# x read in two layouts, and the first pair's projection three token tiles ahead of its attention

## The chip, the cores and the metric

The kernel runs on one core of a Trainium2 chip. The metric is the device time of one execution in microseconds (us); the time before is the median of three runs.

## What is computed

A decoder trunk of two residual layers on x of 1024 tokens by 1024 features, all in float32. Layer 0 mixes tokens with gMLP (A) and with a mixture of dilated sliding-window attentions (B); layer 1 with gated linear attention; each layer ends in a gated MLP with a causal convolution. The change touches the beginning of layer 0. Cut to that, the reference is:

```python
h = rms_norm(x, norm_mix_g[layer]).astype(x.dtype)        # x * rsqrt(mean(x*x) + EPS) * g
z = h @ w_in                                              # columns u, v, q, k, vb
a_out = chunked_gmlp(gelu(u), gelu(v), a_ln_g, a_ln_b, a_ws, a_bs)
qh = rms_norm(heads(q), q_g)                              # 8 heads of 64
kh = rms_norm(heads(k), k_g)
vh = heads(vb).astype(jnp.float32)
for window, dilation in B_BRANCHES:                       # ((128, 1), (512, 4), (2048, 16))
    o_r, l_r = dilated_branch(qh, kh, vh, window, dilation)
...
x = x + concat([a_out, b_out]) @ w_out
x = x + conv_ffn(rms_norm(x, norm_ffn_g[layer]), ...)
```

## The kernel before, in words

Tokens are handled in NT = 8 tiles of P = 128. Every large product is done in three passes over operands that are split into a high and a low part (`split`, L98 to L101: ScalarE writes the high part as float32r, VectorE the rest; `scaled`, L103, does the same for weights and multiplies by a gain). The `hq` tiles hold the split, feature-major x of all tokens: `hq[g][n // 4]` has the four feature blocks of parity g for four token tiles.

**Stage 1, `even` (L509).** For each token tile n, x is loaded token-major (L523), its eight 128x128 blocks are transposed on TensorE into PSUM tiles `pt` (L530), and `split` puts them into `hq` (L531). ScalarE squares the same tile with a running sum (L536), and GpSimd makes of it the reciprocal root mean square `r0[:, n]` (`inv_rms`, L137). r0 isn't applied to `hq`, but to the projections' results.

**Stage 2, `attention` (L643).** The eight heads are four pairs. `project(p)` (L696) has, per token tile, one projection `pj` of 24 matmuls (8 feature blocks in 3 passes, 384 columns: q, k, v of a pair), the QK-norm of its result (L712 to L718: ScalarE, VectorE, GpSimd), the values `vN` (L720, also stored to DRAM, L721), the split of q and k, their transposes `tq` and `tk` (L730, L738), and one attention `unit` of the undilated branch (L670): scores `sc`, exponential on ScalarE (L667), transposes `pP` (L681), and products with the values `po` (L689). `dilated(p)` (L757) is eight more units, `combine` weighs the two. `project(p + 1)` is written behind `dilated(p)`. PSUM's eight banks are: `pt` 2, `sc` 2, `pj` 2, `po` 1, `tq` 1 (L512); `pt` serves x's transposes and `pP`. `qn` has 2 buffers, `vN` 3.

**Stage 3.** `gmlp` (projections `pv`) and `u_proj` (`pu`), 8 tiles of 24 matmuls with 512 columns each, then the output projection and the rest of the trunk.

The program is built with a scheduler that fixes the order of the instructions on each engine; loops are where it starts from, not what stands in the queue at the end. All loads and stores go out from SyncE's queue (SP), in order.

## Time and profile before

| | us |
|---|---|
| median of 3 runs (2170.96 to 2174.12) | 2171.78 |
| the profiled execution | 2173.38 |
| its span, from the first to the last instruction | 2171.7 |
| TensorE (PE) busy | 2138.3 |
| VectorE (DVE) busy | 1533.7 |
| ScalarE (ACT) busy | 1033.9 |
| GpSimd (POOL) busy | 488.9 |

The profile is of one execution. PE's weight loads are shown apart (PEld). An idle time carries the engine that ended it. A timeline merges like instructions: start, length, engine, line, name and count; where the length of a merged row reaches over the start of the next, that is the latency of its last instruction. In a row of a window, `(x66)` counts instructions, and PEclk is the granted TensorE clock as a share.

### The profile page before, as it was taken

How to read it: one execution, taken by the hardware profiler on the slowest of the kernel's cores; microseconds unless marked ns; L12 is line 12 of the kernel's file. 1: busy time of each engine (PE TensorE's matmuls, PEld its weight loads, DVE VectorE, ACT ScalarE, POOL GpSimd, SP SyncE). 2: the span in 40 equal slices, each digit the busy share in tenths (PEclk: the TensorE clock that was granted, in tenths of full speed). 3: DMA queues.
4: the chain of work that ended last, by engine and by line, in shares of the span. 5: the costliest groups of instructions: out<-in, count | busy, mean ns of one | idle time of the engine just before them, and what ended most of it. 6: DMA issues, size and time to landing. Idle time of an engine off the chain costs nothing.

```text
span 2171.7 us, 29864 instructions
## 1 busy us (share of the span) xinstructions
PE 2138.3 (98%) x10508; PEld 1811.4 (83%) x10508; DVE 1533.7 (71%) x2451; ACT 1033.9 (48%) x1998; POOL 488.9 (23%) x519
## 2 busy tenths in 40 slices
PE   8999999999999999999999999999999999999999
PEld 7999988887888888878889888888788888888887
DVE  6566655577887888755577776667788878885554
ACT  6555545355444444444454455534544444444443
POOL 4444411012342434100020011110233424220000
PEclk9999999999999999999999999999999999999999
DMA  4122312655444444675563233386554444457555
GB/s 163 43 83 62 82 51 84 217 207 193 159 151 160 160 165 160 199 266 195 193 215 127 73 98 97 107 295 232 197 165 160 151 152 157 165 181 276 199 196 202
DMA packets 157254, 349.59 MB, mean 161 GB/s; under 512 B 17408, under 2 KB 54272, under 8 KB 156720
## 3 DMA queue, kind: packets, MB, share of 16 engines
q1 hardware_dynamic: 157104, 347.68, 47.6%
q8 instruction: 83, 1.36, 0.3%
q14 instruction: 67, 0.55, 0.1%
HBM read 239.02 MB, written 108.59 MB: 160 GB/s over the span
## 4 chain that ended last, share of the span: by engine, by line
PE 87%; DVE 4%; DMA 4%; ACT 3%; issue 1%; POOL 0%; SPq 0%; ACTq 0%; DVEq 0%; POOLq 0%
PE puB L290 11%; PE pgB L290 11%; PE pv L190 6%; PE pgC L290 6%; PE puC L290 6%; PE pj L190 5%; PE pdB L397 5%; PE pdC L397 5%; PE po L190 4%; PE pdO L397 4%; PE puA L290 3%; PE pgA L290 3%; PE pdP L397 2%; PE pdQ L397 2%; PE pu L190 2%; PE pBq L992 2%
## 5 line engine op out<-in xcount | busy, mean ns | idle before, releaser
L101 DVE TENSOR_TENSOR da<-ar,da 128x512 fp32r<-128x512 f32 x154 | 106.2, 690 | 160.2 <-ACT da L100 160.1
L100 ACT CAST da<-ar 128x512 fp32r<-128x512 f32 x154 | 95.9, 623 | 215.0 <-PE pdQ L397 91.8
L190 PE MATMUL po<-wo,hq 128*128 128x512 f32 x768 | 184.3, 395 | 1.2 <-ACT hq L100 1.2
L190 PEld LDWEIGHTS po<-wo,hq 128*128 128x128 f32 x768 | 141.6, 188 | 30.9 <-ACT hq L100 1.6
L190 PE MATMUL pv<-wv,hq 128*128 128x512 f32 (+2 forms) x768 | 139.8, 339 | 2.0 <-DVE b L1024 1.6
L397 PE MATMUL pdB<-dw,da 128*128 128x512 f32 x528 | 136.3, 391 | 2.4 <-ACT dw L100 1.7
L397 PE MATMUL pdC<-dw,da 128*128 128x512 f32 x528 | 135.8, 390 | 0.0
L190 PEld LDWEIGHTS pv<-wv,hq 128*128 128x128 f32 x768 | 118.9, 189 | 17.4 <-DVE b L1024 2.1
L397 PEld LDWEIGHTS pdB<-dw,da 128*128 128x128 f32 x528 | 98.6, 188 | 24.0 <-ACT dw L100 2.1
L190 PE MATMUL pj<-wq,hq 128*128 128x384 f32 x576 | 117.3, 346 | 0.2 <-ACT vN L720 0.2
L256 POOL TENSOR_TENSOR S1g<-rg 128x512 f32<-128x512 f32 x20 | 30.0, 1498 | 382.9 <-DMA wsd<-D 249.7
L397 PEld LDWEIGHTS pdC<-dw,da 128*128 128x128 f32 x528 | 99.1, 188 | 20.5
L101 DVE TENSOR_TENSOR dw<-wr,dw 128x512 fp32r<-128x512 f32 x154 | 105.6, 686 | 8.2 <-ACT dw L100 7.7
L140 POOL TENSOR_SCALAR rn<-ssq 128x1 f32<-128x1 f32 x24 | 9.6, 399 | 452.2 <-ACT h L148 246.0
L397 PE MATMUL pdO<-dw,da 128*128 128x512 f32 x396 | 102.3, 389 | 0.2 <-DVE dw L101 0.2
L190 PEld LDWEIGHTS pj<-wq,hq 128*128 128x128 f32 x576 | 100.3, 191 | 0.5 <-ACT vN L720 0.4
L100 ACT CAST dw<-wr 128x512 fp32r<-128x512 f32 x154 | 95.0, 617 | 11.9 <-DMA wr<-in_w_dn 5.0
L397 PEld LDWEIGHTS pdO<-dw,da 128*128 128x128 f32 x396 | 74.3, 188 | 15.9 <-DVE dw L101 0.6
L319 DVE SCALAR_TENSOR_TENSOR t<-g,cw,t 128x1022 f32<-128x1022 f32 x44 | 76.6, 1742 | 0.1
L318 DVE SCALAR_TENSOR_TENSOR t<-g,cw,t 128x1023 f32<-128x1023 f32 x44 | 60.2, 1368 | 16.3 <-ACT t L317 16.3
L303 DVE TENSOR_TENSOR g<-g,s1g 128x512 f32<-128x512 f32 x22 | 16.2, 737 | 76.7 <-ACT s1g L302 76.7
L320 ACT ACTIVATE t<-t 128x1024 f32<-128x1024 f32 x44 | 46.7, 1061 | 32.5 <-DVE t L319 32.5
(1073 smaller groups left out, 5458.7 us busy)
## 6 DMA issues: line engine op xcount, KB each, us to landing
ar<-actd SPq DMA_DIRECT2D x70, 512.0 KB, 3.6
rd<-in_w_down SPq DMA_DIRECT2D x44, 512.0 KB, 3.7
wsd<-D SPq DMA_DIRECT2D x88, 256.0 KB, 2.5
rg<-in_w_gate SPq DMA_DIRECT2D x42, 512.0 KB, 3.6
ru<-in_w_up SPq DMA_DIRECT2D x42, 512.0 KB, 4.7
wr<-wsd SPq DMA_DIRECT2D x40, 512.0 KB, 4.3
actd<-t SPq DMA_DIRECT2D x66, 256.0 KB, 2.2
wr<-in_w_dn SPq DMA_DIRECT2D x30, 512.0 KB, 4.6
```

Of the source, the lines that this page charges most:

```text
L100: (hi or A.copy)(dst[0], src)
L101: (lo or V.tensor_sub)(dst[1], src, f32(dst[0]))
L140: G.tensor_scalar(r, ssq, 1.0 / n, EPS, op0=ALU.mult, op1=ALU.add)
L190: T.matmul(o, L[i], R[jj][:, sl], start=(k == 0 and (ii, jj) == PASSES[0]), stop=(k == nk - 1 and (ii, jj) == PASSES[-1]))
L256: G.tensor_tensor(sums[name], x, y, op=op)
L290: T.matmul(o, L[ii][:, j * P : j * P + P], right[p][:, jj, j, :], skip_group_check=more, start=(not more and j == 0 and (ii, jj) == PASSES ...
L303: V.tensor_add(C22, C22, s1)
L318: V.scalar_tensor_tensor(t[:, 1:], g[:, : S - 1], w(1), t[:, 1:], op0=ALU.mult, op1=ALU.add)
L319: V.scalar_tensor_tensor(t[:, 2:], g[:, : S - 2], w(0), t[:, 2:], op0=ALU.mult, op1=ALU.add)
L320: A.activation(t, t, AF.Silu)
L397: T.matmul(o, L[ii][:, t * P : t * P + P], R[jj], skip_group_check=more, start=start and not more and (ii, jj) == PASSES[0], stop=stop and ...
L992: T.matmul(o, L[ii][:, j * P : j * P + P], right[p][:, jj, j, :], skip_group_check=more, start=(not more and j == 0 and (ii, jj) == PASSES ...
```

## The change

The host hands x over a second time, as `x_T`: for each token tile the eight blocks already feature-major, in the order that `hq` wants. Stage 1 loads a tile of `x_T` and splits it straight from SBUF; the 64 transposes of x and their PSUM tiles are gone. For tiles 0 and 1, GpSimd writes the high part of the second half. The token-major x is loaded as well, for the row statistics alone, which are taken in place: of tiles 0 to 2 in stage 1, of tile n + 3 behind the values of projection n.

`project` is split: `projected(n)` has the projection, the QK-norm and the values, and for pair 0 it is called three tiles ahead of the units (`lead = 3`); tiles 1 and 3 of pair 0 use `pt` banks, so that four projections can be under way. For all pairs `qn` now has 5 buffers and `vN` 6, the values are taken before the norm, and the gains `gqk` are kept once and broadcast over the two heads instead of being loaded twice.

```diff
@@ -518,26 +518,57 @@
             wx = par0.enter_context(tc.tile_pool(name="wx", bufs=4, side="right", reuse_waits="tile"))
             pq0 = par0.enter_context(tc.tile_pool(name="pq0", bufs=1, side="right", reuse_waits="tile"))
             with tc.tile_pool(name="nrm", bufs=1, reuse_waits="tile") as pool:
+                Q.dma_start(g0, a["norm_mix_gT"])
+                xk = pq.tile([P, 4, S], F32, tag="kT", bufs=1, name="xk")
+                xq = pq.tile([P, 2, S], F32, tag="qR", bufs=1, name="xq")
+
+                def home(name, tag, bufs):
+                    return pool.tile([P, D], F32, tag=tag, bufs=bufs, name=name)
+
+                def statistics(n, xt):
+                    ssq = small.tile([P, 1], F32, tag="ssq", name=f"ssq{n}")
+                    A.activation(xt, xt, AF.Square, accum_out=ssq)
+                    inv_rms(ssq, 1, D, f"rn{n}", r0[:, n : n + 1])
+
+                def token_rows(n):
+                    xt = home(f"x0{n}", "a", 5) if n < 2 else xk[:, n - 2] if n < 6 else xq[:, n - 6]
+                    Q.dma_start(xt, rows(a["x"], n))
+                    later.append(xt)
+                    if n < 3:
+                        statistics(n, xt)
+
+                later = []
                 for n in range(NT):
-                    xt = pool.tile([P, D], F32, tag="x", bufs=3, name=f"x0{n}")
-                    Q.dma_start(xt, rows(a["x"], n))
+                    xt = home(f"xf{n}", "a", 5) if n < 4 else home(f"xf{n}", "b", 2) if n < 6 else xq[:, n - 6]
+                    xf = xt.rearrange("p (g j t) -> p g j t", g=2, j=4)
+                    Q.dma_start(xf, a["x_T"][n])
+                    for g in range(2):
+                        split(place(hq[g][n // 4], n), xf[:, g], hi=G.tensor_copy if g and n < 2 else None)
                     if n == 0:
-                        Q.dma_start(g0, a["norm_mix_gT"])
-                    for g in range(2):
-                        pt = ps.tile([P, 4, P], F32, tag="pt", name=f"pt{n}{g}")
-                        for j in range(4):
-                            k = 2 * j + g
-                            T.transpose(pt[:, j, :], xt[:, k * P : (k + 1) * P], ident)
-                        split(place(hq[g][n // 4], n), pt)
-                    if n == 1:
                         wq0 = load_qkv(0, wx)
-                    h = pool.tile([P, D], F32, tag="h", bufs=2, name=f"h{n}")
-                    ssq = small.tile([P, 1], F32, tag="ssq", name=f"ssq{n}")
-                    A.activation(h, xt, AF.Square, accum_out=ssq)
-                    inv_rms(ssq, 1, D, f"rn{n}", r0[:, n : n + 1])
+                        token_rows(0)
+                    elif n > 1:
+                        if n == 2:
+                            gqk = gains(pq)
+                        token_rows(n - 1)
+                token_rows(NT - 1)
+
+            def rest(n, ins):
+                if n < 5:
+                    with tc.issue_after(ins.ins):
+                        statistics(n + 3, later[n + 3])
+
             with tc.tile_pool(name="at", bufs=2, reuse_waits="tile") as at, \
                     tc.tile_pool(name="av", bufs=1, reuse_waits="tile") as av:
-                return attention(ps, at, av, pq, pq0, par0, wx, wq0, masks, gm_open)
+                return attention(ps, at, av, pq, pq0, par0, wx, wq0, gqk, masks, rest, gm_open)
+
+    def gains(pq):
+
+        gqk = pq.tile([P, 2, 64], F32, name="gqk", bufs=1)
+        Q.dma_start(gqk[:, 0], a["q_g"].partition_broadcast(P))
+        Q.dma_start(gqk[:, 1], a["k_g"].partition_broadcast(P))
+        V.tensor_scalar(gqk[:, 0], gqk[:, 0], -0.125, None, op0=ALU.mult)
+        return gqk
 
     def band_masks(pool):
 
@@ -640,14 +671,8 @@
 
         proj512(ps, load_half(a["w_vu"][1], "wu", g0), "pu", consume)
 
-    def attention(ps, at, av, pq, pq0, par0, wx, wq0, masks, gm_open):
-
-        gqk = pq.tile([P, 2, 2, 64], F32, name="gqk", bufs=1)
-        for s in range(2):
-            Q.dma_start(gqk[:, 0, s, :], a["q_g"].partition_broadcast(P))
-            Q.dma_start(gqk[:, 1, s, :], a["k_g"].partition_broadcast(P))
-        V.tensor_scalar(gqk[:, 0], gqk[:, 0], -0.125, None, op0=ALU.mult)
-        gqk = gqk.rearrange("p a s c -> p (a s c)")
+    def attention(ps, at, av, pq, pq0, par0, wx, wq0, gqk, masks, rest, gm_open):
+
         mband, mboth = masks
 
         def by4(t):
@@ -693,7 +718,7 @@
             return (at.tile([P, 4, 132], F32, tag="ot", name="ot" + name, bufs=5),
                     ps.tile([P, 4, P], F32, tag="po", name="po" + name))
 
-        def project(p, ws=None, then=None):
+        def project(p, ws=None, then=None, early=None):
 
 
             ws = ws or load_qkv(p, wx)
@@ -701,24 +726,38 @@
             qR = pool.tile([P, 2, S], F32R, tag="qR", bufs=1, name=f"qR{p}")
             kT = pool.tile([P, 4, S], F32R, tag="kT", bufs=1, name=f"kT{p}")
             vd = dram.tile([S, P], F32, name=f"vd{p}")
-            vN, os = [], []
-            for n in range(NT):
-                pj = ps.tile([P, 512], F32, tag="pj", name=f"pj{p}{n}")
+            vN, os, qns = [], [], []
+            heads = lambda t: t.rearrange("p (h c) -> p h c", c=64)
+
+            def projected(n):
+
+                pj = ps.tile([P, 512], F32, tag="pt" if early and n in (1, 3) else "pj", name=f"pj{p}{n}")
                 mm_tok([(pj[:, :384], slice(0, 384))], lambda k: tok(n, k),
                        lambda k: ws[k], KD)
-                qn = pq.tile([P, 256], F32, tag="qn", bufs=2, name=f"qn{p}{n}")
-                heads = lambda t: t.rearrange("p (h c) -> p h c", c=64)
+                qn = pq.tile([P, 256], F32, tag="qn", bufs=5, name=f"qn{p}{n}")
                 rn = r0[:, n : n + 1]
                 A.activation(qn, pj[:, :256], AF.Square, scale=rn)
+                vN.append(pq.tile([P, P], F32, tag="vN", bufs=6, name=f"vN{p}{n}"))
+                got = A.mul(vN[n], pj[:, 256:384], rn)
+                if early:
+                    early(n, got)
+                Q.dma_start(rows(vd, n), vN[n])
                 ssq = small.tile([P, 4], F32, tag="ss4", name=f"ss{p}{n}")
                 V.reduce_sum(ssq, heads(qn), axis=AX.X)
                 r = inv_rms(ssq, 4, 64, f"rq{p}{n}")
                 V.scalar_tensor_tensor(heads(qn), heads(pj[:, :256]), rn, r[:, :, None].to_broadcast([P, 4, 64]),
                                        op0=ALU.mult, op1=ALU.mult)
-                G.tensor_tensor(qn, qn, gqk, op=ALU.mult)
-                vN.append(pq.tile([P, P], F32, tag="vN", bufs=3, name=f"vN{p}{n}"))
-                A.mul(vN[n], pj[:, 256:384], rn)
-                Q.dma_start(rows(vd, n), vN[n])
+                both = qn.rearrange("p (a s c) -> p a s c", a=2, s=2)
+                G.tensor_tensor(both, both, gqk[:, :, None, :].to_broadcast([P, 2, 2, 64]), op=ALU.mult)
+                qns.append(qn)
+
+            lead = 3 if early else 0
+            for n in range(lead):
+                projected(n)
+            for n in range(NT):
+                if n + lead < NT:
+                    projected(n + lead)
+                qn = qns[n]
                 qs = pq.tile([P, 2, P], F32R, tag="qs", bufs=2, name=f"qs{p}{n}")
                 ks = pq.tile([P, 4, P], F32R, tag="ks", bufs=2, name=f"ks{p}{n}")
                 split([qs[:, :, :64], qs[:, :, 64:]], heads(qn[:, :P]), hi=G.tensor_copy)
@@ -798,7 +837,7 @@
             V.tensor_add(o0, o0, o1)
             Q.dma_start(bcat[g].rearrange("(n p) c -> p n c", p=P)[:, :, p * P : p * P + P], o0)
 
-        made = project(0, wq0)
+        made = project(0, wq0, early=rest)
         for p in range(PAIRS):
             os, *qkv = made
             od = dilated(p, *qkv)
@@ -1238,6 +1277,7 @@
     A = {n: np.asarray(v) for n, v in i.items()}
     return {n: c(v) for n, v in {
         "x": A["x"][0],
+        "x_T": A["x"][0].reshape(NT, P, 4, 2, P).transpose(0, 4, 3, 2, 1),
         "norm_mix_g": A["norm_mix_g"][1:],
         "norm_mix_gT": A["norm_mix_g"][0].reshape(KD, P).T,
         "norm_ffn_gT": A["norm_ffn_g"].reshape(2, KD, P).transpose(0, 2, 1),
```

**Place 1, the opening.** SP's queue from its first load, before:

```order
L523 DMA x_324<-in_x 128x1024
L525 DMA g_83<-in_norm_mix_gT 128x8
L523 DMA x_346<-in_x 128x1024
L110 DMA wq00r<-in_w_qkv 128x768
L110 DMA wq01r<-in_w_qkv 128x768
L110 DMA wq02r<-in_w_qkv 128x768
L110 DMA wq03r<-in_w_qkv 128x768
L523 DMA x_399<-in_x 128x1024
L647 DMA gqk<-in_q_g 128x64
L648 DMA gqk<-in_k_g 128x64
L523 DMA x_420<-in_x 128x1024
```

and with the change:

```order
L521 DMA g_83<-in_norm_mix_gT 128x8
L544 DMA xf_327<-in_x_T 128x1024
L110 DMA wq00r<-in_w_qkv 128x768
L110 DMA wq01r<-in_w_qkv 128x768
L110 DMA wq02r<-in_w_qkv 128x768
L110 DMA wq03r<-in_w_qkv 128x768
L535 DMA x_365<-in_x 128x1024
L544 DMA xf_371<-in_x_T 128x1024
L544 DMA xf_377<-in_x_T 128x1024
L568 DMA gqk<-in_q_g 128x64
L569 DMA gqk<-in_k_g 128x64
L535 DMA x_387<-in_x 128x1024
```

One 512 KB load of token-major x and the second one ahead of the weights became one load of `x_T` ahead of them and a load of x behind them; from there on x and `x_T` alternate. TensorE at the end of the second projection (`pj_617` is tile 1 of pair 0, `pj_695` tile 2), before:

```order
L190 MATMUL pj_617<-wq_1_391,hq_87 128x384
L530 MATMUL pt_422<-ident,x_420 128x128 x4
L190 MATMUL pj_617<-wq_1_391,hq_87 128x384 x2
L530 MATMUL pt_429<-ident,x_420 128x128 x4
L530 MATMUL pt_443<-ident,x_441 128x128 x4
L190 MATMUL pj_695<-wx_364,hq_85 128x384 x3
```

and at the end of the fourth (`pj_564`), with the change:

```order
L190 MATMUL pj_564<-wq_0_359,hq_85 128x384 x3
L190 MATMUL pj_564<-wq_1_362,hq_87 128x384 x3
L769 MATMUL tq_611<-identr,qs_605 128x128 x2
L190 MATMUL pj_644<-wx_335,hq_86 128x384 x3
L190 MATMUL pj_644<-wx_338,hq_88 128x384 x3
```

Before, groups of four transposes of x stand between the projections; now they follow one another, with the first transposes of q (`tq_611`) behind the fourth.

**Place 2, the end of pair 0's projections.** ScalarE's queue there, before (`wx` and `wq` are weights of the next pairs, `qT_978` is the transposed q of tile 5):

```order
L105 ACTIVATE wx_2234<-wq20r,g_83 128x384
L105 ACTIVATE wx_2237<-wq20r,g_83 128x384
L105 ACTIVATE wx_2242<-wq21r,g_83 128x384
L105 ACTIVATE wx_2245<-wq21r,g_83 128x384
L105 ACTIVATE wq_0_1371<-wq12r,g_83 128x384
L105 ACTIVATE wq_1_1374<-wq12r,g_83 128x384
L105 ACTIVATE wq_0_1379<-wq13r,g_83 128x384
L733 CAST qT_978<-tq_975 128x256
```

and with the change (`qT_772` is that of tile 2, `qn_829` the square of projection 6's result):

```order
L739 ACTIVATE qn_829<-pj_804,r_84 128x256
L105 ACTIVATE wx_2154<-wq20r,g_83 128x384
L105 ACTIVATE wx_2157<-wq20r,g_83 128x384
L105 ACTIVATE wx_2162<-wq21r,g_83 128x384
L105 ACTIVATE wx_2165<-wq21r,g_83 128x384
L105 ACTIVATE wq_0_1291<-wq12r,g_83 128x384
L105 ACTIVATE wq_1_1294<-wq12r,g_83 128x384
L772 CAST qT_772<-tq_769 128x256
```

The scaling of the next pairs' weights now stands ahead of tile 2's q instead of tile 5's. TensorE, before (`pj_1088` is pair 0's last projection, `pj_1388` pair 1's first):

```order
L190 MATMUL pj_1088<-wq_1_391,hq_88 128x384 x2
L681 MATMUL pP0n_909<-ident,sm0n_921 128x128 x2
L190 MATMUL pj_1088<-wq_1_391,hq_88 128x384
L738 MATMUL tk_981<-identr,ks_970 128x128 x4
L689 MATMUL po0n_908<-vN_807,pT0n_926 128x64
L689 MATMUL po0n_908<-vN_886,pT0n_926 128x64
L689 MATMUL po0n_908<-vN_807,pT0n_926 128x64
L689 MATMUL po0n_908<-vN_886,pT0n_926 128x64
L190 MATMUL pj_1388<-wq_0_1355,hq_85 128x384 x3
```

and with the change (`pj_883` is pair 0's last projection):

```order
L190 MATMUL pj_883<-wq_1_362,hq_88 128x384 x3
L777 MATMUL tk_775<-identr,ks_764 128x128 x4
L706 MATMUL pP0n_703<-ident,sm0n_707 128x128 x2
L706 MATMUL pP0n_703<-ident,sm0n_715 128x128 x2
L686 MATMUL sc0n_782<-kT_439,qT_772 128x256 x2
L686 MATMUL sc0n_790<-kT_439,qT_772 128x256 x2
L769 MATMUL tq_847<-identr,qs_841 128x128 x2
L714 MATMUL po0n_624<-vN_468,pT0n_720 128x64
L714 MATMUL po0n_624<-vN_509,pT0n_720 128x64
L714 MATMUL po0n_624<-vN_468,pT0n_720 128x64
L714 MATMUL po0n_624<-vN_509,pT0n_720 128x64
L777 MATMUL tk_853<-identr,ks_842 128x128 x4
```

Before, one unit's end stands between the pairs' projections; now units 1 to 3 do, with rows 83 to 99 of TensorE's queue, and pair 1's first projection follows at row 100.

**Place 3, the late units of pair 1** (names with 1n; `pj_2267` and `pj_2343` are projections of pair 2). TensorE, before:

```order
L190 MATMUL pj_2267<-wq_1_2261,hq_87 128x384 x3
L661 MATMUL sc1n_1867<-kT_1386,qT_1857 128x256 x2
L661 MATMUL sc1n_1875<-kT_1386,qT_1857 128x256 x2
L730 MATMUL tq_1932<-identr,qs_1926 128x128 x2
L738 MATMUL tk_1938<-identr,ks_1927 128x128 x4
L681 MATMUL pP1n_1866<-ident,sm1n_1870 128x128 x2
L681 MATMUL pP1n_1866<-ident,sm1n_1878 128x128 x2
L661 MATMUL sc1n_1945<-kT_1386,qT_1935 128x256 x2
L661 MATMUL sc1n_1953<-kT_1386,qT_1935 128x256 x2
L730 MATMUL tq_2010<-identr,qs_2004 128x128 x2
L689 MATMUL po1n_1771<-vN_1749,pT1n_1883 128x64
L689 MATMUL po1n_1771<-vN_1845,pT1n_1883 128x64
```

and with the change (`pj_2187` and `pj_2263` are projections of pair 2):

```order
L686 MATMUL sc1n_1787<-kT_1306,qT_1777 128x256 x2
L686 MATMUL sc1n_1795<-kT_1306,qT_1777 128x256 x2
L769 MATMUL tq_1852<-identr,qs_1846 128x128 x2
L190 MATMUL pj_2187<-wq_1_2181,hq_87 128x384 x3
L190 MATMUL pj_2263<-wx_2154,hq_85 128x384 x3
L190 MATMUL pj_2263<-wx_2157,hq_87 128x384 x3
L190 MATMUL pj_2263<-wx_2162,hq_85 128x384 x3
L190 MATMUL pj_2263<-wx_2165,hq_87 128x384 x3
L190 MATMUL pj_2263<-wq_0_2170,hq_85 128x384 x3
L190 MATMUL pj_2263<-wq_1_2173,hq_87 128x384
```

Before, the units of tiles 5 to 7 stand together between two projections; with the change a projection stands between any two of them.

## The prediction, made blind

> **What bounds the kernel now.** I read the page's first and fourth parts, then the windows of the beginning, then TensorE's timeline there.
>
> ```profile
> PE 2138.3 (98%) x10508; PEld 1811.4 (83%) x10508; DVE 1533.7 (71%) x2451; ACT 1033.9 (48%) x1998; POOL 488.9 (23%) x519
> PE 87%; DVE 4%; DMA 4%; ACT 3%; issue 1%; POOL 0%; SPq 0%; ACTq 0%; DVEq 0%; POOLq 0%
> ```
>
> TensorE is the bound: 98% busy, and 87% of the chain that ended last. So an edit is worth what it takes off TensorE's queue, plus the time in which TensorE waits or runs thin. Where is that? Per window, PE busy with its count, then the other engines, granted clock, DMA share and GB/s:
>
> ```profile
> 0.00:10.00 10.00, 3.56 (x14) 2.74 (x15) 5.27 (x15) 5.74 (x10) 3.06 (x13) 1.00 0.78 275
> 10.00:20.00 10.00, 10.00 (x49) 9.93 (x48) 7.62 (x15) 9.11 (x18) 1.49 (x4) 1.00 0.90 318
> 20.00:30.00 10.00, 8.76 (x60) 8.38 (x59) 6.09 (x13) 7.29 (x18) 7.52 (x16) 1.00 0.59 198
> 70.00:80.00 10.00, 9.51 (x57) 8.84 (x56) 5.20 (x16) 3.94 (x12) 4.71 (x8) 0.83 0.22 70
> ```
>
> The first 20 us are poor (14 and 49 matmuls where dense windows have over 70) and the DMA engines are nearly full there. At 70 to 80 the clock was 0.83. Now single stretches of TensorE, chosen from its timeline (length, busy, count, clock):
>
> ```profile
> 41.34:49.82 8.48, 6.83 (x55) 1.00 0.01 3
> 65.87:69.66 3.79, 2.03 (x16) 1.00 0.79 219
> 69.66:74.80 5.14, 5.14 (x20) 0.67 0.46 148
> 75.40:80.69 5.29, 4.69 (x37) 1.00 0.00 0
> 141.99:148.03 6.04, 4.93 (x38) 1.00 0.26 86
> 208.20:211.80 3.60, 2.58 (x18) 1.00 0.39 137
> 110.51:121.88 11.37, 10.83 (x94) 1.00 0.33 85
> ```
>
> To see what they lost I need a step per matmul. From two dense places:
>
> ```profile
> 61.34 2.24 PE L190 MATMUL pj<-wx,hq 128*128 128x384 f32 x12
> 63.42 1.74 PE L190 MATMUL pj<-wq,hq 128*128 128x384 f32 x9
> ...
> 84.09 0.63 PE L661 MATMUL sc0n<-kT,qT 128*128 128x256 f32 x4
> 84.56 1.00 PE L689 MATMUL po0n<-vN,pT0n 128*128 128x64 f32 x8
> 85.37 0.34 PE L730 MATMUL tq<-identr,qs 128*128 128x128 f32 x2
> ```
>
> A projection matmul takes (63.42 - 61.34) / 12 = 0.173 us, a token tile's 24 so 4.15 us; a small one of a unit (85.37 - 84.09) / 12 = 0.107 us. At these steps the stretches lost: 41.34: 8.48 - 55 x 0.107 = 2.6. 65.87: 3.79 - 0.17 - 15 x 0.107 = 2.0. 69.66: twenty projection matmuls should take 3.46, so 1.7, by the clock of 0.67. 75.40, with four projection matmuls: 5.29 - 0.69 - 33 x 0.107 = 1.1. 141.99: 2.0. 208.20: 1.7. 110.51: 1.3, or 0.014 us per instruction. **Pair 0 loses 7.4 us (the first four), the late units of pairs 1 and 2 lose 3.7 us.**
>
> **The transposes of x.**
>
> ```profile
> L530 PE MATMUL pt<-ident,x 128*128 128x128 f32 x64 | 11.4, 312 | 6.7 <-DMA x<-in_x 5.5 <-DVE hq L101 1.2
> L530 PEld LDWEIGHTS pt<-ident,x 128*128 128x128 f32 x64 | 8.7, 160 | 7.6 <-issue 4.6 <-DVE hq L101 2.7
> ...
> 34.78 0.53 PEld L530 LDWEIGHTS pt<-ident,x 128*128 128x128 f32 x4
> ...
> 35.27 2.06 PEld L190 LDWEIGHTS pj<-wx,hq 128*128 128x128 f32 x12
> ```
>
> The 312 ns mean holds latency; between dense neighbours four take 35.27 - 34.78 = 0.49 us, so 64 cost 7.8 us of TensorE's queue. They are work on the bounding engine, so they go for good, but the first of them stand beside a wait for data; so the opening is priced as a whole.
>
> **The opening.**
>
> ```profile
> 1.70 5.56 DMA x<-in_x
> ...
> wq00r<-in_w_qkv SPq DMA_DIRECT2D x1, 384.0 KB, 6.1
> ...
> wq03r<-in_w_qkv SPq DMA_DIRECT2D x1, 384.0 KB, 7.6
> ```
>
> ```profile
> 2.16 0.43 SPq L110 DMA_DIRECT2D wq00r<-in_w_qkv  x1
> 3.58 0.92 SPq L110 DMA_DIRECT2D wq03r<-in_w_qkv  x1
> 9.47 0.69 PE L190 MATMUL pj<-wx,hq 128*128 128x384 f32 x1 [0.99 <-ACT wx L105]
> 10.66 4.83 PE L190 MATMUL pj<-wx,hq 128*128 128x384 f32 x14
> 21.96 0.60 PE L190 MATMUL pj<-wq,hq 128*128 128x384 f32 x2
> 22.39 0.60 PE L530 MATMUL pt<-ident,x 128*128 128x128 f32 x4
> ```
>
> The second 512 KB of x landed at 1.70 + 5.56 = 7.26, the first weights at 2.16 + 6.1 = 8.26, the fourth at 3.58 + 7.6 = 11.18: 384 KB per 0.97 us, so 512 KB per 1.3. With the change one 512 KB load instead of two stands ahead of the weights: they land at about 6.9 to 9.9, x tile 0 at 11.2, the second x_T tile at 12.5, the third at 13.9. ScalarE scales the first weights 0.6 us after they land, so the first projection matmul starts at 7.6 instead of 9.47. The first 14 ran at 4.83 / 14 = 0.345 us, twice the later step: TensorE was slow until about 15.5, 6 us after 9.47. Give the change the same 6 us: 17 slow matmuls until 13.5, by when the second tile is there (12.5, and about 1.3 for its split). The other 55 of three tiles take 55 x 0.173 = 9.5, until 23.0. So at 22.5 some 69 matmuls are done. Before, at 22.5 (the rows at 21.96 and 22.39) two tiles were done, 48 matmuls, with seven groups of four transposes. **The gain is 21 x 0.173 + the other 36 transposes at 0.122 = 3.6 + 4.4 = 8.0 us.** Bounds: 3.6 + 4.4 - 3 if the DMAs are so late that the second projection waits 3 us more (8.4 MB of x and x_T at the 318 GB/s of the window need 26 us, from tile 3 on each lands over 4 us ahead of its turn), and 8.0 + 1.2 if the clock rises after 3.4 us.
>
> The Trainium skill (TensorE: Matmul & The Clock Gate, Part 1) says that TensorE starts at half clock and is released after some 3.4 us of sustained activity. This trace has the half rate, but for 6 us; by the page's figure the opening would gain 1.2 us more, an estimate that I leave out.
>
> **What is moved to GpSimd and ScalarE.**
>
> ```profile
> L718 POOL TENSOR_TENSOR qn<-qn,gqk 128x256 f32<-128x256 f32 x13 | 9.8, 753 | 7.8 <-DVE qn L716 5.5 <-PE sc1n L661 0.9 <-PE pP0n L681 0.7
> ...
> L796 POOL TENSOR_TENSOR ot0n<-ot0n,cE 128x512 f32<-128x512 f32 x2 | 2.6, 1298 | 9.2 <-DVE cE L793 9.2
> ...
> L536 ACT ACTIVATE h<-x 128x1024 f32<-128x1024 f32 x8 | 8.5, 1058 | 5.6 <-DMA x<-in_x 5.5
> ```
>
> The multiplication by broadcast gains is not in the trace; the row at L796 broadcasts too and takes 1298 ns for twice the elements, so between 650 and 753 ns: no change. The eight squares stay at 1.06 us each, in place. The split's second half on GpSimd for two tiles saves ScalarE two casts of 0.6 us that nobody waits for. The extra DMA issues of SP are ahead of nothing that is due before 27. All this I cost at 0, covered by projections 1 to 5, in which TensorE waits for nothing else; if a bank isn't freed in time there, each 1 us of delay costs 1 us.
>
> **The units of pair 0 behind its projections.** From 23.0 TensorE has projections 3, 4, 5 with q's and k's transposes until 35.6, projection 6 with unit 0's first scores until 40.8, projection 7 until 45.9. Then rows 84 to 99 of its queue: units 1 to 3 without any projection, some 40 instructions, 4.3 us. There the chain of ScalarE counts.
>
> ```profile
> L105 ACT ACTIVATE wq<-wq11r,g 128x384 fp32r<-128x384 f32 x2 | 1.1, 619 | 0.0
> ...
> L666 DVE CUSTOM_DVE_ANT_1 sm0n<-sc0n,mband 128x256 f32<-128x256 f32 x14 | 8.2, 619 | 7.4 <-PE sc0n L661 7.4
> L667 ACT ACTIVATE sm0n<-sm0n,ot0n 128x256 f32<-128x256 f32 x14 | 7.1, 508 | 6.3 <-DVE ot0n L666 6.3
> ...
> 66.91 0.50 PE L738 MATMUL tk<-identr,ks 128*128 128x128 f32 x4 [0.62 <-ACT qT L733]
> ```
>
> Six weights (0.56 each back to back, 1.1 us for two) stand ahead of tile 2's qT, two more between its exponentials; each unit then goes round scores, 0.62 on VectorE, 0.51 on ScalarE, transposes, copy, and waits for kT behind them. Walked through, scores of unit 2 come at 49.9, of unit 3 at 52.7, pair 1's first projection at 53.7: 7.8 us for 4.3 of work, 3.5 lost. The row at 66.91 is this same wait of before, behind the same eight weights. Units 5 and 6 lose another 1.0 near 68. So pair 0 loses 4.5 instead of 7.4: **2.9 us gained**, which counts on the slow clock of 69.66 (1.7) not returning.
>
> **The late units of pairs 1 and 2.**
>
> ```profile
> ACT vN L720 <- PE po0n L689: 8.7, 4, 3.5
> ```
>
> In the first 130 us the values waited four times, 8.7 us, for products with older values: three buffers held the projections back behind the units, so that a pair's last three projections and its last units came late. Six take that away. In TensorE's order projections of the next pair now stand between units 5, 6 and 7, so the stretches at 141.99 and 208.20 should fill: **3.7 us**. The stretch like 110.51 becomes longer, 150 instructions without a projection instead of 135: at its 0.014 us that is 0.2 us a pair, 0.6 in all; at the price of 141.99 (2.0 / 38 = 0.053) it would be 2.4. I take 0.6, from the row of the same kind of stretch.
>
> **Sum.** 8.0 + 2.9 + 3.7 - 0.6 = 14.0. The walk has no time for handing over between engines, so I take 13. Behind the output projection the order of each engine is as before, so the gain carries through. Against the profiled execution: 2173.4 - 13 = 2160.4; that execution was 1.6 above the median, so **2159 us** beside the median.
>
> **The rivals.** (1) **The clock falls again.** The row at 70 to 80 (0.83) follows a thin stretch, 2.03 us busy of 3.79. With the change 46 to 50 is thinner: 0.5 us of work in 3.6. A fall costs 5.14 - 3.46 = 1.7, giving 2160.7. For: the mechanism is in the trace; against: once only, and 41.34 didn't bring it. The Trainium skill (the same page, Why this matters for your kernels) says that an idle of more than about 3 us between bursts of matmuls sends the clock back to half. This trace agrees with the price, though its stretch was thin, not empty. (2) **Only the opening is gained**, because the scheduler's new order has as many waits as the old one: about 2165, from 8.0 less some late casts. For: the same DVE and ACT work has to fit; against: three and six buffers, above. (3) **x_T comes late**, the second to fourth projections wait for DMAs that share the full engines, and each 1 us is lost: with 5 us more, and no gain at the units, 2169, no measurable change. (4) **Slower: units without projections run at the price of 141.99.** The change has some 40 + 3 x 150 = 490 such instructions; at 0.053 instead of 0.014 they lose 19 us, against 14 gained: 2177. It decides from 0.043 us each. Against: 110.51 is just such a stretch and lost 0.014.
>
> **How the numbers follow.** Forecast 0.45, (1) 0.25, (2) 0.18, (3) 0.07, (4) 0.05. The range of 2153 to 2167.5 takes in the first three, the upper bound of the opening (1.2), and 4 us more should the new order also remove small waits. 0.2%, 4.3 us, is about what a measurement can tell from no change. Faster: 0.45 + 0.25 + 0.15 of (2) = 0.85; same 0.10; slower 0.05.
>
> **What would show it.** PE's first projection matmul at 7.6; three projections done at 23; no L530 transposes; pair 1's first projection near 53.7 (before 69.66); no stretch like 141.99 in pairs 1 and 2; no wait of vN for po. Wrong would be a PE wait for DMA xf behind 14 us, or pair 1's first projection after 60.

## The result, and the profile after

The changed kernel took 2162.53 us (median of 5 runs, 2161.23 to 2163.74), the kernel before 2172.2 us beside it (5 runs, 2170.96 to 2174.71): ratio 0.9942, 95% interval 0.993 to 0.9955, so 10 to 15 us less (12.6 by the ratio; the medians lie 9.7 apart). The profiled execution took 2161.23 us, with a span of 2159.5 against 2171.7. Forecast were 2159 for the median and 2160.4 for the profiled execution.

First, where the time was gained. The output projection's transposes of `cat` close layer 0's mixing; in a tile's view, their line gives the first and the last start. Before:

```profile
L442 PE MATMUL pc<-ident,cat x96: 270/272/299, 384.1 to 1472.6; 128*128 128x128 f32 x96
```

After:

```profile
L442 PE MATMUL pc<-ident,cat x96: 270/272/301, 372.9 to 1459.8; 128*128 128x128 f32 x96
```

They start 11.2 us earlier, and the span is 12.2 shorter: nearly all of the gain lies ahead of 373 us, where the prediction had it. TensorE's windows of the kernel after (length, busy with its count, granted clock, DMA share, GB/s):

```profile
0.00:22.50 22.50, 15.52 (x68) 1.00 0.87 328
30.00:40.00 10.00, 8.42 (x54) 1.00 0.77 246
40.00:50.00 10.00, 9.53 (x65) 1.00 0.33 100
50.00:60.00 10.00, 8.99 (x66) 1.00 0.34 94
...
70.00:80.00 10.00, 9.59 (x72) 1.00 0.02 7
120.00:140.00 20.00, 17.67 (x117) 0.91 0.30 80
140.00:160.00 20.00, 20.00 (x138) 1.00 0.04 11
200.00:220.00 20.00, 19.87 (x139) 1.00 0.14 41
```

At 22.5 us 68 projection matmuls are done (69 were forecast). The clock's fall at 70 us is gone (0.83 before, 1.00 now), and the poor stretches of before at 142 and 208 us are full. But there are two holes that the prediction did not have, at 30 to 40 and at 120 to 140 us, the second with a clock of 0.91. TensorE's and its neighbours' rows at the first hole (start, length, what; in brackets the idle time before and what ended it):

```profile
34.93 0.41 DVE L746 TENSOR_REDUCE ss<-qn 128x4 f32<-128x256 f32 x1
...
35.32 1.14 POOL L751 TENSOR_TENSOR qn<-qn,gqk 128x256 f32<-128x256 f32 x1
...
36.54 0.39 POOL L140 TENSOR_SCALAR rq<-ss 128x4 f32<-128x4 f32 x1
36.60 0.47 ACT L739 ACTIVATE qn<-pj,r 128x256 f32<-128x256 f32 x1 [2.35 <-POOL qn L751]
...
37.01 1.07 POOL L141 TENSOR_TENSOR rq<-rq,mhalf 128x4 f32<-128x4 f32 x1
...
38.12 0.48 DVE L748 SCALAR_TENSOR_TENSOR qn<-pj,r,rq 128x256 f32<-128x256 f32 x1 [0.91 <-POOL rq L141]
...
38.66 1.66 PE L190 MATMUL pj<-wx,hq 128*128 128x384 f32 x8 [1.58 <-DVE qn L748]
```

Read from the bottom: the next projection waits 1.58 us for a bank, which VectorE's norm frees, which waits for GpSimd's `rq`. The sums `ss` that `rq` needs were there at 35.34 (34.93 + 0.41), but GpSimd was at the multiplication by the gains for the tile before, until 36.46. ScalarE's 2.35 us are put down to the same multiplication, but they don't belong to this chain: the projection that its square reads ended only at 36.52 (its last 12 matmuls start at 34.25 and take 2.27 us). GpSimd was busy for 9.20 us of 20 to 30 and for 9.16 of 30 to 40 (7.52 and 6.54 before):

```profile
20.00:30.00 10.00, 9.20 (x16) 1.00 1.02 399
30.00:40.00 10.00, 9.16 (x15) 1.00 0.77 246
```

The second hole, on VectorE, SyncE's queue and TensorE:

```profile
121.05 1.87 SPq L847 DMA_DIRECT2D on<-od  x2
...
124.29 0.17 DVE L818 TENSOR_TENSOR cM<-ot0n,on 128x8 f32<-128x8 f32 x1 [2.60 <-DMA on<-od]
...
124.65 0.60 DVE L691 CUSTOM_DVE_ANT_1 sm1n<-sc1n,mband 128x256 f32<-128x256 f32 x1
...
125.94 0.69 PE L706 MATMUL pP1n<-ident,sm1n 128*128 128x128 f32 x2 [2.17 <-ACT sm1n L692]
```

The merge of pair 0's halves (`combine`, called at tile 3 of pair 1's projection) begins with a small VectorE operation on `on`, which comes back from DRAM by a load that was issued only at 121.05. VectorE takes its queue in order and stands for 2.60 us; behind it stands the masking of pair 1's scores (L691), and TensorE waits 2.17 us for what follows from that. In the kernel before, the same operation had nothing to wait for:

```profile
118.05 1.26 SPq L808 DMA_DIRECT2D on<-od  x2
...
121.07 0.17 DVE L779 TENSOR_TENSOR cM<-ot0n,on 128x8 f32<-128x8 f32 x1
```

VectorE came to it at 121.07 there and at 121.69 (124.29 - 2.60) here, nearly the same time; it is the load that moved, from 118.05 to 121.05. The merges of the later pairs waited before, too (0.87 and 3.45 us on VectorE, at 188 and 257 us), but TensorE had other work there. Right behind the wait at 124 us, from 125.82 to 129.23, the granted clock is 0.50: 11 instructions in 3.41 us.

```profile
125.82:129.23 3.41, 3.28 (x11) 0.50 0.08 24
```

Last, the waits that were to vanish, between 60 and 250 us (times in us, how often, the longest):

```profile
DVE qn L748 <- ACT vN L741: 11.4, 5, 3.2
...
ACT vN L741 <- PE po0n L714: 7.7, 3, 3.3
```

The values still wait for products with older values (10.1 us in four waits from the start on, 8.7 before): it is pair 1's first values that wait, at 59 to 85 us, for pair 0's units. And now the norm waits for the values, too.

### The profile page after: what moved, and what is told of

It reads as the page before. It is cut to its first block, busy times and chain, and to the rows that moved or that the text cites. A ratio compares the mean times of both kernels' runs of the same rounds, so it can differ in the third digit from the quotient of the medians.

```text
span 2159.5 us, 29700 instructions
## 1 busy us (share of the span) xinstructions
PE 2128.4 (99%) x10444; PEld 1803.4 (84%) x10444; DVE 1528.3 (71%) x2451; ACT 1036.3 (48%) x1998; POOL 489.6 (23%) x521
## 4 chain that ended last, share of the span: by engine, by line
PE 84%; DVE 5%; DMA 5%; ACT 3%; issue 1%; POOL 1%; SPq 0%; DVEq 0%; ACTq 0%; POOLq 0%
PE puB L290 11%; PE pgB L290 11%; PE pgC L290 6%; PE puC L290 6%; PE pdB L397 5%; PE pdC L397 5%; PE pj L190 5%; PE pv L190 5%; PE pdO L397 4%; PE po L190 3%; PE puA L290 3%; PE pgA L290 3%; PE pdP L397 2%; PE pdQ L397 2%; PE pu L190 2%; PE pBr L1031 2%
```

## The experiments

All medians are in us; since the kernel before came out between 2172.2 and 2175.9 beside them, kernels are compared by their ratio to it, the changed kernel at 0.9942. Behind each ratio stands its 95% interval. Where an interval overlaps that of the changed kernel (0.993 to 0.9955), the two times aren't told apart, and for the changed kernel itself the quotient of the medians, 0.9955, lies 3 us above the ratio. The lines of code are the changed kernel's unless said otherwise.

**1. The feed alone.** No lead, two banks, old buffer counts; the values stay ahead of the norm.

```diff
-            lead = 3 if early else 0
+            lead = 0
-                pj = ps.tile([P, 512], F32, tag="pt" if early and n in (1, 3) else "pj", ...)
+                pj = ps.tile([P, 512], F32, tag="pj", ...)
-                qn = pq.tile([P, 256], F32, tag="qn", bufs=5, ...)
+                qn = pq.tile([P, 256], F32, tag="qn", bufs=2, ...)
-                vN.append(pq.tile([P, P], F32, tag="vN", bufs=6, ...))
+                vN.append(pq.tile([P, P], F32, tag="vN", bufs=3, ...))
```

> The changed kernel's opening alone: x_T is loaded and split, and x's rows follow for the statistics, but pair 0's projection stands in its unit again (lead 0), in the two pj banks, with the old buffers (qn 2, vN 3). Theory T (the feed is worth about 8 us by itself, the lead and the buffers are small and partly given back at 36.8 and 123.5 us): about 2165 us (2163 to 2167), with pair 0's units losing as much as before (about 7 us). Rival L (the gain comes from the projections that run ahead, and the transposes that went lay in waits for data that remain): about 2170 us (2168.5 to 2172).

Measured: 2206.6, ratio 1.0149 (1.0132 to 1.0165): 32 us **slower** than before, and neither theory had it. The trace shows a chain that the old order didn't have:

```profile
154.05 1.10 PE L714 MATMUL po1n<-vN,pT1n 128*128 128x64 f32 x8
...
154.97 0.37 ACT L741 ACTIVATE vN<-pj,r 128x128 f32<-128x128 f32 x1 [0.19 <-PE po1n L714]
...
155.37 0.48 DVE L748 SCALAR_TENSOR_TENSOR qn<-pj,r,rq 128x256 f32<-128x256 f32 x1 [1.68 <-ACT vN L741]
...
155.91 0.79 PE L190 MATMUL pj<-wx,hq 128*128 128x384 f32 x3 [0.23 <-DVE qn L748]
```

An older unit's products free a `vN` buffer, the value copy follows, then the norm, and then the bank for the next projection. With three buffers a projection is tied to a unit's end, and VectorE waited for the values 15 times in the first 380 us:

```profile
DVE qn L748 <- ACT vN L741: 31.0, 15, 4.0
```

A part of the loss is clock: in this profile the granted clock is at half in five places before 425 us, some 20 us in all, which costs half of that, 10 us.

**2. The lead alone.** The opening of before (x turned by TensorE), and the changed `project` with its lead, banks and buffers.

```diff
-                    xf = xt.rearrange("p (g j t) -> p g j t", g=2, j=4)
-                    Q.dma_start(xf, a["x_T"][n])
+                    xt = pool.tile([P, D], F32, tag="x", bufs=3, name=f"x0{n}")
+                    Q.dma_start(xt, rows(a["x"], n))
...
+                            T.transpose(pt[:, j, :], xt[:, k * P : (k + 1) * P], ident)
```

> The kernel before's opening (x is turned by TensorE, 64 transposes) with the changed projection: three tiles ahead, four banks, qn 5, vN 6. Theory T: the first projection matmul stays near 9.5 us and the opening term of 8 us is missing; the rest is worth 1 to 4 us, so 2168 to 2171 us. Rival L: about 2164 us (2162 to 2166), since the lead is what gains.

Measured: 2179.66, ratio 1.002 (1.0008 to 1.0031), 2 to 7 us **slower** than before. Both missed. At 33 and 35 us TensorE waits 0.97 and 1.17 us for VectorE's splits of x; here these also free the two `pt` banks, which x's transposes share with the projections of tiles 1 and 3, and the rows don't tell which of the two mattered. The larger losses are the merge's, as in the changed kernel:

```profile
133.62 0.17 DVE L797 TENSOR_TENSOR cM<-ot0n,on 128x8 f32<-128x8 f32 x1 [2.23 <-DMA on<-od]
...
135.24 0.74 PE L665 MATMUL sc1n<-kT,qT 128*128 128x256 f32 x4 [2.04 <-DVE kT L757]
```

The next pair's merge does the same (2.93 us on VectorE, 2.00 us on TensorE, at 203 us), and the output projection waits 3.01 us for `cat` at 388 us. Behind each of the three the clock falls (0.91 in each of the windows 120 to 140, 200 to 220 and 380 to 400 us), and once more at 1467 us. So this run doesn't show that the lead and the buffers are worth nothing by themselves; it shows them together with a merge that stops TensorE.

**3. The feed and the buffers.** Run 1 with `qn` 5 and `vN` 6; no lead, two banks.

> As the run with the feed alone, with the buffers of the change besides (qn 5, vN 6), still without a lead and in two banks. Theory T: the late units of pairs 1 and 2 gain their 3 to 4 us from the buffers, pair 0's units lose what they lost before (about 3 us more than in the changed kernel) but the wait at 36.8 us (1.6 us) is not there: within 2 us of the changed kernel, 2161 to 2165 us. Rival L: about 2169 us, as the feed alone less a little. If the late units' gain doesn't hang on the buffers, the same time as the feed alone, within 0.5 us.

Measured: 2166.9, ratio 0.9962 (0.9947 to 0.9977), some 40 us less than run 1: the buffers pay for the moved values. The median is 2 us above Theory T's range, by the ratio it is within it (0.9962 x 2172.2 = 2163.9), and its interval overlaps the changed kernel's. Values that wait for pair 0's units are down to 1.8 us in two waits. The windows of pair 0:

```profile
10.00:20.00 10.00, 7.53 (x31) 0.84 0.95 375
...
30.00:40.00 10.00, 9.50 (x60) 1.00 0.76 226
40.00:50.00 10.00, 10.00 (x68) 1.00 0.14 43
50.00:60.00 10.00, 9.99 (x72) 1.00 0.53 164
0.00:60.00 60.00, 50.55 (x291) 0.97 0.69 246
```

Without a lead, the first 60 us hold 291 instructions, 216 of them projection matmuls; with it 292 and 212. The lead fills 10 to 20 us (47 against 31) and gives it all back between 30 and 60 (185 against 200). What lies above the changed kernel is later:

```profile
180.00:200.00 20.00, 17.81 (x127) 0.91 0.45 127
360.00:380.00 20.00, 17.14 (x76) 0.96 0.44 144
```

TensorE waits behind two merges (1.93 us at 124.86 and 1.85 at 192.92) and 2.37 us for `cat` at 377, and this profile has four falls of the clock in all, the changed kernel's one.

**4. Two banks.** The changed kernel, with `tag="pj"` for all of pair 0's projections.

> The changed kernel with the first pair's projections in the two pj banks alone; the lead of three stays. Theory T (the four banks cover the QK-norm's latency while projections run back to back, and GpSimd at 4.2 us a tile is the limit there either way): 0 to 2 us slower than the changed kernel, 2162.5 to 2164.5 us, with TensorE's waits for a bank between 14 and 40 us. Rival: with two banks each projection waits for the norm of the second before it, 3 to 4 us of latency for each of five or so tiles that have only the next projection to run meanwhile, and the lead is worth nothing: 2168 us or more.

Measured: 2162.66, ratio 0.9941 (0.9927 to 0.9955): four banks are worth nothing that shows. The waits for the norm are still there with two banks, smaller and more of them (0.30, 0.97 and 0.41 us), and GpSimd is as busy (9.29 of 20 to 30 us):

```profile
30.71 2.39 PE L190 MATMUL pj<-wx,hq 128*128 128x384 f32 x12 [0.97 <-DVE qn L748]
```

**5. The feed with the values where they were.** Run 1, with the value copy and its store behind the multiplication by the gains again.

> The x_T feed with the projection as it was: no lead, two banks, qn 2, vN 3, and the values taken behind the norm again (the gains stay the narrow broadcast ones). Theory V (the earlier run with the feed alone lost 30 us because the value copy stands ahead of the norm there and waits for a vN buffer, and with it the norm, the bank and the next projection): that loss is gone and what is left is the opening's 8 us, 2164 to 2169 us. Rival Q (the loss came from the feed itself, by x's later rows, the statistics or the narrow gains): 2190 us or more.

Measured: 2168.59, ratio 0.9974 (0.9963 to 0.9984). Theory V holds: run 1's loss was the order of the values, and the feed by itself gains 5.6 us (3.5 to 8.0), a little under the 8.0 of the opening. In this profile the clock stands at half for 6.8 us, behind thin units of pair 0, which costs 3.4 of the gain there:

```profile
40.00:50.00 10.00, 9.14 (x41) 0.66 0.28 82
```

**6. Six value buffers alone in run 1.** `vN` 6, `qn` still 2.

> The run with the feed alone (no lead, two banks, qn 2, values ahead of the norm) with vN 6 in place of 3 and nothing else. Theory V: the 40 us that lay between that run and the one with both buffer counts come from vN, so 2164 to 2171 us. Rival N (qn's two buffers held the projections back): over 2195 us. Half of each would give about 2185 us.

Measured: 2164.75, ratio 0.9959 (0.9947 to 0.9972), as run 3. All of the 40 us came from `vN`; more `qn` buffers are worth nothing that shows here.

**7. The buffers alone in the kernel before.**

```diff
-                qn = pq.tile([P, 256], F32, tag="qn", bufs=2, ...)
+                qn = pq.tile([P, 256], F32, tag="qn", bufs=5, ...)
-                vN.append(pq.tile([P, P], F32, tag="vN", bufs=3, ...))
+                vN.append(pq.tile([P, P], F32, tag="vN", bufs=6, ...))
```

> The kernel before with qn 5 and vN 6 buffers and nothing else; its values stay behind the norm. The prediction's term for the late units (vN's buffers free the copy from the unit two back, 3.7 us): about 2168 us. Theory V (in the old order a value copy that waits holds nothing that TensorE needs soon, and the buffers only pay for the move of the copy): within 2 us of the kernel before, either way, 2170 to 2175 us.

Measured: 2168.73, ratio 0.9974 (0.9963 to 0.9984), a gain of 5.6 us: the prediction's term holds, and Theory V was wrong to give the buffers nothing in the old order. The stretches at 142 and 208 us are full, as forecast, and a new hole in pair 3 takes a part back:

```profile
0.00:80.00 80.00, 71.61 (x459) 1.00 0.42 139
...
140.00:160.00 20.00, 20.00 (x134) 1.00 0.10 28
...
200.00:220.00 20.00, 20.00 (x140) 1.00 0.09 27
...
240.00:260.00 20.00, 17.45 (x121) 0.88 0.68 231
```

The first line is the surprise: with x still turned by TensorE, 459 instructions are done at 80 us; before, it was 423:

```profile
0.00:80.00 80.00, 68.41 (x423) 0.98 0.40 133
```

Of these, 277 against 216 are projection matmuls, 118 against 143 the small ones of the units, and 64 in both the transposes of x: at the prediction's steps of 0.173 and 0.107 us that is 61 x 0.173 - 25 x 0.107 = 7.9 us more work by then, an estimate. So the stretch of pair 0's units gains from the buffers alone, with no lead, and the clock doesn't fall at 70. The units themselves end later (their last scores start at 90.9 us, before at 84.4): projections of pair 1 stand between them.

**8. The merge two tiles later.**

```diff
-                if then and n in (3, 4):
-                    then(n - 3)
+                if then and n in (5, 6):
+                    then(n - 5)
```

> The changed kernel with the merge of the previous pair's halves two tiles later (tiles 5 and 6 in place of 3 and 4). Theory D (VectorE's in-order wait for the transfer od to on holds TensorE for 2.3 us at 123.5 us, and the clock falls behind that stretch, 1.7 us): the wait for on goes and the clock stays up, 3 to 5 us less than the changed kernel, 2157.5 to 2159.5 us. Rival: the merge's vector and GpSimd work (some 4 us of it for each half) now falls on units that have no slack, and it is the same or up to 3 us slower, 2162 to 2166 us.

Measured: 2158.65, ratio 0.9927 (0.9915 to 0.994), 3.3 us under the changed kernel by the ratios, as Theory D had it, but the intervals overlap, so the size isn't settled by this run alone (run 9 against run 3 is the same edit, and clear). The mechanism is in the trace: VectorE no longer waits for `on` in the first 380 us (6.1 us in three waits in the changed kernel), the first merge starts at 131.59, and the window is full at full clock:

```profile
120.00:140.00 20.00, 19.76 (x145) 1.00 0.34 92
```

**9. The same without the lead.** Run 3 with the late merge.

> The feed and the buffers without a lead and in two banks, as in an earlier run (2166.9 us), with the merge two tiles later. Theory W (the lead itself is worth nothing; the 4 us between the changed kernel and that earlier run are clock falls behind thin stretches, which stood elsewhere): as the changed kernel with the late merge, 2157 to 2161 us. Rival L (the lead is worth about 4 us by its fuller first units): 2161.5 to 2165 us.

Measured: 2158.07, ratio 0.9925 (0.9912 to 0.9938), the same as run 8, and 8 us under run 3, clear of noise. Theory W holds: the lead and the four banks are worth nothing that shows here; what run 3 lost were the holes at the merges and the clock's falls, of which this profile has none before 2150 us. Its five runs lay between 2157.69 and 2159.2, all with a mean clock of 0.999 or 1.000.

**10. The feed and the buffers in the old order.** Run 5 with `qn` 5 and `vN` 6.

> Two parts alone: the x_T feed (5.7 us by itself, by ratio) and the buffers qn 5, vN 6 (5.7 us by itself); the values stay behind the norm, no lead, two banks, the merge where it was. If the parts add, the ratio to the kernel before is 0.9948, some 2161 to 2163 us, as much as the whole change (0.9942), and neither the lead nor the move of the values is worth anything. If the lead or the move carries a part of the change's gain: 2165 us or more.

Measured: 2163.16, ratio 0.9948 (0.9935 to 0.996), the sum of runs 5 and 7 (that it agrees to the digit is luck, the intervals are 5 us wide), and the whole change is at 0.9942. Within the noise these two parts are the whole change; the lead, the banks and the move of the values add nothing that shows.

**11. The gains on VectorE for pair 0, with the late merge.**

```diff
-                G.tensor_tensor(both, both, ...)
+                (V if early else G).tensor_tensor(both, both, ...)
```

> The changed kernel with the late merge and with the first pair's multiplication by the gains on VectorE in place of GpSimd. Theory G (between 20 and 40 us GpSimd, at 4.2 us a tile, holds the norms, the banks and so the projections back; 0.9 us a tile less of it frees TensorE from the 1.6 us wait at 36.8 us): 1 to 2 us less than with the late merge alone, 2156 to 2158 us. Rival: VectorE's row is as full there, or the wait goes over to the next one behind it: within 0.5 us of the late merge alone, or slower.

Measured: 2157.26, ratio 0.9919 (0.9907 to 0.9931), inside Theory G's range, but the trace speaks against it: the wait is there still, and GpSimd's `rq` still ends it.

```profile
35.16 0.41 DVE L746 TENSOR_REDUCE ss<-qn 128x4 f32<-128x256 f32 x1
...
35.65 0.83 POOL L140 TENSOR_SCALAR rq<-ss 128x4 f32<-128x4 f32 x1 [1.69 <-DVE ss L746]
...
36.56 1.27 POOL L141 TENSOR_TENSOR rq<-rq,mhalf 128x4 f32<-128x4 f32 x1
...
37.87 0.48 DVE L748 SCALAR_TENSOR_TENSOR qn<-pj,r,rq 128x256 f32<-128x256 f32 x1 [0.92 <-POOL rq L141]
...
38.41 1.83 PE L190 MATMUL pj<-wx,hq 128*128 128x384 f32 x9 [1.37 <-DVE qn L748]
```

GpSimd now waits 1.69 us for VectorE's sums: in VectorE's queue these stand behind the scaling of the next pair's weights (L106, 1.37 us from 33.53 on) and the multiplication that was moved there, and VectorE is busy for 2.47 of the 2.60 us from 33.00 on. That is the rival's second half: the wait has gone over to the next engine. (ScalarE's 2.35 us are there as well, without a multiplication on GpSimd.) The 1.4 us between the medians of runs 8 and 11 are within both intervals, and run 8's profile has two falls of the clock where this one has none. This is the lowest median of all, 5 us under the changed kernel, but not told apart from runs 8 and 9.

**12. Run 10 with the late merge.**

> The feed and the buffers alone (values behind the norm, no lead, two banks), with the merge two tiles later: of the change only two parts are left. If the move of the values and the lead are worth nothing once the merge holds nobody up: 2156 to 2160 us, with the thin stretch near 250 us and the clock's fall behind it gone. If the move of the values is what fills pair 3's units near 250 us (there the feed and the buffers alone lost 7.3 us in 20, the changed kernel 3.4): 2161 us or more.

Measured: 2161.48, ratio 0.9946 (0.9932 to 0.9959); single runs from 2154.95, the lowest of any kernel, to 2165.98. Inconclusive: by the median the second theory comes true by half a us, but its interval covers both. In the profiled execution, the lowest, the thin stretch near 250 us is gone, as the first theory had it: it had a mean clock of 1.000 and a fuller pair 3 (19.14 of 20 us busy between 240 and 260, 17.57 in run 10); the others had clocks of 0.998 and 0.996. Why the clock falls in this order and not in run 9's is open.

## Why the prediction was right, point by point

The total was right; of its terms, some were too high and some too low, and that they cancelled is luck.

**The opening, 8.0 us: right in size.** 68 matmuls at 22.5 us against 69, and no transposes. Alone, the feed measured 5.6 (3.5 to 8.0). A part of the 68 is the lead's: without it, 53 and 59 are done at 22.5 us (runs 3 and 9), and by 60 us the difference is gone. TensorE started at 6.63 instead of 7.6. Its matmuls were slow until about 13 (the first 12 went from 6.63 to 11.14, 0.376 us each); the granted clock of the windows reads 1.00 there all the same, so only the steps show the slow rate. In run 3 they were faster from about 10.5 on, and TensorE then waited 2.31 us for the second tile's split: data bounds that run's opening, so the earlier rise brought nothing there. Leaving out the 1.2 us was right for this run at least.

**Moves costed at 0: wrong by some 1.6 us.** "TensorE waits for nothing else" in projections 1 to 5 held only to 36.8 us. The multiplication by the gains took 914 ns at 20 to 50 us instead of 650 to 753, and GpSimd set the pace. The step that failed is that GpSimd's row was never added up: projections run back to back ask for a norm every 4.15 us, and GpSimd's means in that stretch (`rq` 0.38 and 1.16, the gains 0.91, the two casts of q and k 0.36 and 0.42, x's statistic 0.25 and 0.55) make 4.0, and 4.9 with a cast of `qR` (0.86). Taking the multiplication away was not enough, though: in run 11 VectorE's row, as full, held `rq` and the bank.

```profile
L141 POOL TENSOR_TENSOR rq<-rq,mhalf 128x4 f32<-128x4 f32 x6 | 7.0, 1163 | 0.4
L751 POOL TENSOR_TENSOR qn<-qn,gqk 128x256 f32<-128x256 f32 x6 | 5.5, 914 | 0.4 <-DVE qn L748 0.4
```

**Pair 0's units, 2.9 us: too low (4.0 below, under "The sum"), and the cause wrong.** The walk gave pair 1's first projection at 53.7; it came at 54.88, and units 1 to 3 lost as walked:

```profile
51.29 0.74 PE L686 MATMUL sc0n<-kT,qT 128*128 128x256 f32 x4 [0.90 <-ACT kT L778]
...
54.88 1.29 PE L190 MATMUL pj<-wq,hq 128*128 128x384 f32 x6
```

But that is the lead's doing, and pair 0 gains as much or more without it (runs 3, 7 and 9): with the lead, what 10 to 20 us gain is lost again between 30 and 60. What helps pair 0 are the buffers (run 7), in the new order `vN` by itself (run 6).

**The late units, 3.7 us: the size right, the reason half right.** The buffers alone gained 5.6 (3.5 to 8.0), in pair 0 as well, with 142 and 208 filled. "Six take that away", the waits of vN for po, is wrong for the changed kernel: with pair 0's projections done early, pair 1's come beside pair 0's units and want the buffers that these still read (10.1 us of waits; 1.8 without the lead, run 3). And the prediction gave no price to the values' move ahead of the norm, which makes the norm and the bank wait with them: 38 us at three buffers (run 1 against run 5), covered by six.

**Not in the sum: the merge.** With the new order the load for pair 1's first merge goes out 3 us later, VectorE gets to the merge as early as before, and TensorE needs what stands behind it: 2.2 us of waiting and a clock's fall of 1.7, in a place other than rival (1) had it. Moving the merge was worth 3.3 us in run 8 and 8 in run 9 against run 3, where two merges cost TensorE time. Rival (1)'s mechanism and price were right (3.41 us at half clock), its place was not.

**The sum.** 13 was taken and 12.2 came out of the profiled span. How far ahead the changed kernel is can be estimated from the instructions that TensorE has begun by a given time, at the prediction's steps (0.173 us for a projection matmul, 0.107 for a small one, 0.122 for a transpose of x):

| until (us) | before: projection, small, transposes of x | changed: projection, small | ahead (us) |
|---|---|---|---|
| 22.5 | 48, 0, 29 | 68, 0 | 7.7 |
| 80 | 216, 143, 64 | 282, 146 | 11.7 |
| 120 | 312, 341, 64 | 384, 334 | 11.7 |
| 140 | 399, 380, 64 | 437, 398 | 8.5 |
| 220 | 624, 708, 64 | 687, 720 | 12.2 |

(At 22.5 us the 35 transposes still to come in the kernel before are counted as gained.) So by this estimate the opening gave 7.7 us where the prediction had 8.0. Pair 0 gave 4.0, with the 1.6 us wait at 36.8 us in it, and 5.6 without; the prediction had 2.9. The stretch of the merge took 3.2, which the prediction did not have, and the late units gave 3.7 where it had 3.7 - 0.6. What pair 0 gave beyond its term and the two missed holes nearly balance.

Rival (2), only the opening, is spoken against by the 4.0 and 3.7 us behind it. Of rival (3) there is a trace: TensorE's wait for the second tile's split is 0.35 us in the changed kernel, but 0.9 to 2.3 us in runs 3, 4, 6, 8 and 11. Rival (4)'s long thin units did not appear.

**Open.** What the lead is worth without the feed once the merge is out of the way (run 2 with the late merge was not run); run 12's falls of the clock. VectorE's scaling of the gains waits 1.81 us for their load at 15.05 us, ahead of three splits of x; an earlier load wasn't tried.

## What to carry to other kernels

Before a copy is moved ahead of the step that frees a shared bank, ask what the copy itself waits for: its buffer count becomes the bank's (some 40 us here, nothing that showed with twice the buffers). Work that runs ahead only moved its wait here, because GpSimd's time per tile was as long as TensorE's, and VectorE's row was as full behind it: add up the other engines' rows first. When the order changes, look at when the loads go out: a small operation that waits for one in an engine's queue held everything behind it (VectorE 2.60 us, TensorE 2.17). And a total that comes out right is no proof of its terms: compare the work done at several times.

## What the runs showed of the hardware

In the 14 profiles of this case the granted clock fell to half 23 times before 2150 us, 19 times for 3.41 us and four times for twice that. The Trainium skill (TensorE: Matmul & The Clock Gate, Part 1) has a free-running window of 3413 ns; the length agrees. The stretches ahead of the falls were thin and not empty: the longest single wait of TensorE there was 3.01 us (run 2), and at 124 us in the changed kernel 2.17 were enough. The same wait does not always bring a fall: behind the 1.58 us at 38.6 us the clock stayed up in the changed kernel and was at half for 3.41 us in run 8.

The times go with the mean clock: over the runs of the kernel before beside the experiments, the median was 2172.9 us at a mean clock of 0.999 or 1.000 (23 runs), 2174.7 at 0.998 (15), 2175.9 at 0.997 (9) and 2178.0 at 0.996 (4). So an edit that removes a thin stretch can gain twice, the wait and the fall behind it, as at 124 us in run 8. Run 9's five runs, all at 0.999 or 1.000, lay within 1.5 us, run 12's, at 0.996 to 1.000, within 11; that a kernel without falls repeats better is suggested by this and not shown.
